# Two gained float32 tiles behind each output product instead of three, with the next norm's second half under a dense tile

## The chip, the cores and the metric

The kernel runs on one core of a Trainium2 chip. The metric is the device time of one execution in microseconds, lower is better.

## The reference

Two decoder layers over 512 prompt tokens and 8 sample tokens (one new token each), all in float32. Cut to what bears on the change:

```python
def rmsnorm(x, g):
    y = xf * lax.rsqrt(jnp.mean(xf * xf, axis=-1, keepdims=True) + EPS)
    return y * g

def decoder_layer(x, ...):
    m, mix_state = gated_parallel_mixer(rmsnorm(x, p['norm_mix_pre']), ...)   # ends in (...) @ w_out
    x = x + rmsnorm(m, p['norm_mix_post'])
    x = x + rmsnorm(cross_attention(rmsnorm(x, p['norm_x_pre']), ...), p['norm_x_post'])
    f, new_buf_ffn = conv_ffn(rmsnorm(x, p['norm_ffn_pre']), buf_ffn, p)
    x = x + rmsnorm(f, p['norm_ffn_post'])

def cross_attention(h, mem_k, mem_v, p):
    q = h @ p['w_xq']          # 8 tiles of 128 columns; softmax attention over 256 memory rows
    ...
    return o @ p['w_xo']

def conv_ffn(h, buf, p):
    a, g = split_cols(h @ p['w_ffn_in'], (D_FF, D_FF))   # 22 tiles each
    ...                        # causal convolution of a, silu, times g
    return (...) @ p['w_ffn_out']
```

So twice in each layer an output product (`w_out`, `w_xo`) is followed by a norm, a residual sum, a second norm of the new x, and at once by the next product (`w_xq`, `w_ffn_in`). These four places are what the change touches.

## The kernel before

Channels lie on the 128 partitions; the 520 tokens lie along the row in two halves of 260 (256 prompt tokens and 4 sample tokens each). A product is made tile by tile: one tile is 128 output columns, summed over the 128-row blocks k of the input.

**Dense tiles** (`dense`, `mm3`). Float32 accuracy is reached with the faster type float32r: weight and input are each split into a high and a low part, and three products (high x high, high x low, low x high) are summed. For 8 blocks and two halves that is 48 matmuls of 260 columns. `load_w` brings the raw weight in over SP's queue, ScalarE makes the high part (L169), VectorE the low part (L111). The pools hold three raw and four split weights. A dense tile's two halves lie in one `pd` buffer of PSUM, of which there are two; `ps` buffers (one bank) are four.

**Behind an output product** (`post`, `late`, `after_norm`). `post` evacuates the eight tiles of the output product into `mg`, sums their squares (`sums`), and forms the first norm's factor in two halves: `Rms` sums the squares over partitions with three small matmuls on TensorE (L267, "stat"), VectorE scales the sum (L250 `nms`), GpSimd raises it to the power -1/2 (L251 `ny`, "newton"), TensorE spreads it over partitions (L275), ScalarE copies it to SBUF (L277 `r`). `bulk(hf)` then makes the new x of one half on VectorE: 8 x (multiply by r, L335; add the residual `xo`, L338), written over `mg`. The second norm's factor r2 needs the squares of the new x: `squares(hf)` takes 8 squares on ScalarE and adds 7 of them (L296) on VectorE.

So that TensorE has work in this time, `after_norm` starts the next product with **three tiles in plain float32**: their weights are multiplied by the norm's gain on ScalarE (`load_wg`, 8 `wg` activations a tile), their input is the new x as it stands, unsplit, and the factor r2 is multiplied in at evacuation. One tile is 8 blocks x 2 halves = 16 matmuls (L407). Between the six (tile, half) groups `after_norm` calls `next(late)`, which emits the parts of `late` one after another: first norm's second half, `bulk(1)`, squares of half 0; r2 of half 0; squares of half 1, and so on; the splits of the new x for the dense tiles (`sph` on ScalarE, `spl` on VectorE) come last, ahead of r2's second half. Behind the three tiles the other tiles (`xq(3)`..., or `wf[NFF+1]`...) are dense.

A scheduler then sets each engine's order from these emissions; semaphores keep it. What the engines do is in that fixed order.

```python
                for k in range(8):
                    PE.matmul(ps[:, :HALF], ws[i][:, k], x[k][:, hf], start=(k == 0), stop=(k == 7))
                wait.append((i, ps, hf))
                next(late)
```

Of the kernel before, what the change touches and what calls it, by code (L numbers as in the profile page):

```python
# [23 lines left out]
NFF = DFF // P  # L24
# [41 lines left out]
def build(tc, I, O):  # L66
# [7 lines left out]
    with ExitStack() as es:  # L74
# [29 lines left out]
        G = nc.gpsimd  # L104
# [12 lines left out]
        def AV(t, hf=None):  # L117

            return t[:, :, :HALF] if hf is None else t[:, hf, :HALF]
# [75 lines left out]
                        PE.matmul(ps, a[:, k], b[:, hf], start=(first and k == 0 and i == 0),  # L195
                                  stop=(last and k == nk - 1 and i == 2))

        def dense(ap, xs):

            kt = len(xs)  # L200
            ps = PD()
            outs = [(ps[:, hf, :HALF], hf) for hf in range(2)]
            for k0 in range(0, kt, 8):
                k1 = min(kt, k0 + 8)
                mm3(load_w(ap[:, k0:k1], k1 - k0), xs[k0:k1], outs, k0 == 0, k1 == kt)
            return ps

        def window(aps, xs, mid=()):
# [91 lines left out]
        def post(w, xs_, gain, src, keep, nwin, nxt=None, final=False):  # L300

            sums = Sum()
            mg = [None] * 8

            def evac(m, ps, hf):
                if mg[m] is None:
                    mg[m] = C("mg")
                v = ps[:, :HALF] if hf is not None else AV(ps)  # L310
                sums.add(v, hf)
                act(AV(mg[m], hf), v, AF.Identity, scale=gain(m))

# [12 lines left out]
            rm, rm2 = {}, {}  # L326

            def stat(hf):
                rm[hf] = Rms(sums.acc, D, hf)

            def bulk(hf):
                for m in range(8):
                    x = AV(mg[m], hf)
                    E = G if not nxt and m in (2, 3) else V
                    E.tensor_tensor(out=x, in0=x, in1=AV(r, hf), op=ALU.mult)  # L335
                    if final and m % 2 == 0:
                        yo = C("yo")
                    E.tensor_tensor(out=yo[:, m % 2] if final else x, in0=x, in1=xo[m][hf], op=ALU.add)  # L338
                    if final and m % 2:
                        nc.sync.dma_start(out=keep[:, m - 1:m + 1, hf], in_=yo)  # L340

            def store():
                for m in range(8):
                    G.dma_start(out=keep[:, m], in_=mg[m])

            def squares(hf):
                for m in range(8):
                    sq2.add(AV(mg[m], hf), hf)

            def late():  # L350
                rm[1].spread(r)
                bulk(1)
                squares(0)
                yield
                rm2[0] = Rms(sq2.acc, D, 0)
                squares(1)
                yield
                rm2[0].spread(r2)
                yield
                rm2[1] = Rms(sq2.acc, D, 1, pd=rm2[0].pd)  # L360
                for m in range(8):
                    split_to(sp[m][0], sp[m][1], mg[m], nxt(m))
                yield
                rm2[1].spread(r2)
                yield
                store()
                yield

            mid = [lambda: None, lambda: stat(0), lambda: rm[0].spread(r)] if nwin == 1 else []
            for n, (i, ps, hf) in enumerate(window([w[m] for m in range(8 - nwin, 8)], xs_, mid)):  # L370
                evac(8 - nwin + i, ps, hf)
                if nwin > 1 and n == nwin:
                    stat(0)
                if nwin > 1 and n == nwin + 1:
# [12 lines left out]
            bulk(1)  # L387
            if not final:
                store()
            return mg  # L390

        def after_norm(aps, x, gain, late, evac):


            n = len(aps)
            ws = [load_wg(ap, 8, gain) for ap in aps]
            pd = None
            wait = []
            for j in range(2 * n):
                hf, i = divmod(j, n)  # L400
                if j < 4:
                    ps = PS()
                else:
                    pd = pd or PD()
                    ps = pd[:, j % 2]
                for k in range(8):
                    PE.matmul(ps[:, :HALF], ws[i][:, k], x[k][:, hf], start=(k == 0), stop=(k == 7))  # L407
                wait.append((i, ps, hf))
                next(late)
                while j >= n and wait and wait[0][2] == 0:  # L410
                    evac(*wait.pop(0))
            for v in wait:
                evac(*v)

        def drain(gen):
            while True:
# [119 lines left out]
        for L in range(DEPTH):  # L536
# [866 lines left out]
            def xq(m):  # L1403
                xq_evac(m, dense(I["w_xq"][L, m], xss), None)

            load_mem(0)
            for h in range(3):
# [3 lines left out]
                                          lambda m: pc("xpre", m)))  # L1411
            x_src = keep

            after_norm([I["w_xq"][L, m] for m in range(3)], x, lambda k: pc("xpre", k), late, xq_evac)
            s_load("mem_v", 0, 0)
            p_scores(0)
            s_scores(0, 0)
            s_load("mem_k", 3, 0)
# [92 lines left out]
            def ffn_g(j, ps, hf):  # L1511
                if j not in gth:
                    gth[j] = C("gg", (P, 512))
                tt(QV(gth[j], hf), PV(r, hf), PV(ps, hf), ALU.mult)
                tt(S8(g_s[:, j], hf), SV(r, hf), SV(ps, hf), ALU.mult)
                if hf is None and j > 1:
                    ffn_mul(j)

            def ffn_mul(j):
# [20 lines left out]
            wf = I["w_ffn_in"][L]  # L1540

            def first(i, ps, hf):
                (ffn_a, ffn_g, ffn_a)[i]((0, 0, 1)[i], ps, hf)

            after_norm([wf[0], wf[NFF], wf[1]], x, lambda k: pc("ffnpre", k), late, first)
            for j in range(1, NFF):
                if j > 1:
                    ffn_a(j, dense(wf[j], xss), None)
                ps = dense(wf[NFF + j], xss)
                ffn_g(j, ps, None)  # L1550
                if j == 1:
                    for i in range(2):
                        ffn_conv(i)
                        ffn_mul(i)
                if j == 8:
                    ffn_sample(0, 8)
                if 9 <= j < 17:
# [210 lines left out]
```

## Time and profile before

| | us |
|---|---|
| median of 3 runs | 3201.71 (3200.33 to 3203.3) |
| the profiled execution | 3205.31 |
| its span | 3203.5 |
| TensorE busy | 3160.6 (99%) |
| VectorE busy | 1949.0 (61%) |
| ScalarE busy | 1454.4 (45%) |
| GpSimd busy | 423.9 (13%) |

Busy times are those of the span, which is 1.8 us shorter than the execution's own time. A matmul's record is longer than the step to the next matmul, because matmuls overlap; what a matmul costs is read from the step between starts. A plain float32 matmul leaves two records, a float32r matmul one.

### The profile page before, as it was taken

To read this page: it belongs to the slowest core of one execution; us is meant where nothing else is said; L and a number is where in the kernel's file an instruction comes from. 1 tells how busy PE (TensorE), PEld (TensorE's weight loads), DVE (VectorE), ACT (ScalarE), POOL (GpSimd) and SP (SyncE) were. 2 spreads that over 40 slices of the span, in tenths; PEclk is the share of its full clock that TensorE was granted. 3 is DMA by queue.
4 is the path that set the end of the run, shared out by engine and by line. 5 is a ranking of instruction groups with operands and counts; after the bars stand their busy time and mean duration, and the time that the engine had idled before them with its cause. 6 is when DMAs were issued, how large, how long until landed. Compare 5 with 4: busy or idle time off the path is not lost. (4 is left out here: it accounts for less than half of the span.)

```text
span 3203.5 us, 64089 instructions
## 1 busy us (share of the span) xinstructions
PE 3160.6 (99%) x25878; PEld 3020.2 (94%) x25878; DVE 1949.0 (61%) x3773; ACT 1454.4 (45%) x3348; POOL 423.9 (13%) x762
## 2 busy tenths in 40 slices
PE   8999999999999999999999999999999999999998
PEld 7989999999999879999999899999999998899998
DVE  6665686777553537665286666777775436376643
ACT  5343566666433434333243445676673233433331
POOL 1100222122300101000020011222223001010001
PEclk9999999999999999999999999999999999999999
DMA  7322444444643553223263234444455336432231
GB/s 258 122 83 100 140 166 150 146 162 160 215 139 107 186 172 127 96 96 109 88 228 110 80 103 162 158 140 160 153 183 197 123 109 213 147 129 96 94 96 64
DMA packets 192168, 445.83 MB, mean 139 GB/s; under 512 B 26416, under 2 KB 78656, under 8 KB 191872
## 3 DMA queue, kind: packets, MB, share of 16 engines
q1 hardware_dynamic: 162736, 353.63, 33.0%
q0 software_dynamic: 27840, 86.01, 7.9%
q8 instruction: 203, 3.33, 0.4%
q10 hardware_dynamic: 1296, 2.11, 0.2%
q14 instruction: 93, 0.76, 0.1%
HBM read 377.81 MB, written 63.83 MB: 138 GB/s over the span
## 5 line engine op out<-in xcount | busy, mean ns | idle before, releaser
L169 ACT CAST wh<-wr 128x1024 fp32r<-128x1024 f32 (+1 forms) x484 | 503.4, 1041 | 1139.6 <-PE pd L195 763.9
L111 DVE TENSOR_TENSOR wl<-wr,wh 128x1024 fp32r<-128x1024 f32 (+1 forms) x484 | 591.4, 1223 | 523.3 <-ACT wh L169 514.4
L195 PE MATMUL pd<-xih,wh 128*128 128x260 f32 x3488 | 716.8, 287 | 3.2 <-ACT dd L108 3.2
L195 PE MATMUL pd<-xih,wl 128*128 128x260 f32 x3488 | 702.6, 283 | 0.0
L195 PE MATMUL pd<-xil,wh 128*128 128x260 f32 x3488 | 702.1, 283 | 0.0
L195 PEld LDWEIGHTS pd<-xih,wh 128*128 128x128 f32 x3488 | 536.8, 189 | 25.3 <-issue 19.2
L195 PEld LDWEIGHTS pd<-xih,wl 128*128 128x128 f32 x3488 | 537.7, 188 | 0.1
L195 PEld LDWEIGHTS pd<-xil,wh 128*128 128x128 f32 x3488 | 537.6, 189 | 0.1
L195 PE MATMUL pd<-sph,wh 128*128 128x260 f32 x1472 | 298.0, 284 | 0.0
L195 PE MATMUL pd<-spl,wh 128*128 128x260 f32 x1472 | 296.4, 283 | 0.0
L195 PE MATMUL pd<-sph,wl 128*128 128x260 f32 x1472 | 295.8, 282 | 0.0
L195 PEld LDWEIGHTS pd<-sph,wh 128*128 128x128 f32 x1472 | 226.8, 188 | 2.9 <-issue 2.7
L195 PEld LDWEIGHTS pd<-spl,wh 128*128 128x128 f32 x1472 | 227.9, 189 | 0.0
L195 PEld LDWEIGHTS pd<-sph,wl 128*128 128x128 f32 x1472 | 226.7, 188 | 0.1
L114 DVE SCALAR_TENSOR_TENSOR cv<-pb,hw,cv 128x512 f32<-128x512 f32 x192 | 143.6, 748 | 5.5 <-ACT cv L108 0.7
L251 POOL TENSOR_TENSOR ny<-nms,mhalf 128x3 f32<-128x3 f32 (+2 forms) x26 | 39.2, 1506 | 787.6 <-DVE nms L250 787.6
L195 PE MATMUL pd<-uh,wh 128*128 128x260 f32 x616 | 124.1, 283 | 0.0
L195 PE MATMUL pd<-uh,wl 128*128 128x260 f32 x616 | 123.9, 282 | 0.0
L195 PE MATMUL pd<-ul,wh 128*128 128x260 f32 x616 | 123.6, 282 | 0.0
L108 ACT ACTIVATE th<-cv 128x512 f32<-128x512 f32 x64 | 40.5, 633 | 154.4 <-DVE cv L114 133.0
L296 DVE TENSOR_TENSOR acc<-acc,sq 128x260 f32<-128x260 f32 (+1 forms) x126 | 61.8, 513 | 76.6 <-ACT sq L108 75.2
L195 PEld LDWEIGHTS pd<-ul,wh 128*128 128x128 f32 x616 | 95.1, 188 | 0.0
(425 smaller groups left out, 6052.1 us busy)
## 6 DMA issues: line engine op xcount, KB each, us to landing
wr<-in_w_in SPq DMA_DIRECT2D x218, 512.0 KB
wr<-in_w_ffn_in SPq DMA_DIRECT2D x88, 512.0 KB
hs<-in_ssm SPq DMA_DIRECT2D x64, 256.0 KB
csb<-csd SPq DMA_DIRECT2D x64, 256.0 KB
out_s_ssm<-hs POOLq DMA_DIRECT2D x64, 256.0 KB, 2.8
mem_k<-in_mem_k SPq DMA_DIRECT2D x64, 256.0 KB
wr<-in_w_ssm_out SPq DMA_DIRECT2D x32, 512.0 KB
mem_v<-in_mem_v SPq DMA_DIRECT2D x64, 256.0 KB
```

The costliest lines, as they stand in the source:

```text
L108: return A.activation(out, in_, f, **kw)
L111: return V.tensor_tensor(out=out, in0=a, in1=b, op=op)
L114: return V.scalar_tensor_tensor(out=out, in0=a, scalar=s, in1=b, op0=op0, op1=op1)
L169: A.copy(h[:, :nk], raw[:, :nk])
L195: PE.matmul(ps, a[:, k], b[:, hf], start=(first and k == 0 and i == 0), stop=(last and k == nk - 1 and i == 2))
L251: G.tensor_tensor(out=y, in0=ms, in1=mhalf[:, 0:n], op=ALU.pow)
L296: (E or V).tensor_tensor(out=AV(self.acc, h), in0=AV(self.acc, h), in1=AV(sq, h), op=ALU.add)
```

## The change

- `after_norm` takes **two** gained tiles instead of three (32 plain matmuls instead of 48 at each place), all four (tile, half) groups in `ps` buffers. The calls of `next(late)` stand inside the groups. It returns `rest`, which emits the last part of `late` and the evacuation of half 1.
- The third tile becomes a **dense** tile: `xq(2)`, or `wf[1]`. `dense` and its callers take `mid`: after 3 of 8 blocks it calls `rest`, that is, r2's second half (stat, newton, spread) and `store`.
- In `late` the splits of the new x come **first**, ahead of the squares of half 1; the squares of half 0 come before `bulk(1)`.
- The 7 additions of squares of each half go to **GpSimd** (`E=G`) instead of VectorE: 14 additions of 128x260 at each place, 56 in all.
- In the ConvFFN the convolution of tile 0 is emitted behind the dense tile `wf[1]`, and `ffn_g` of every tile calls `ffn_mul`.

The lines of the changed kernel are shifted: the additions of squares are L303, the stat L274, `nms` L257, `ny` L258, the spread L282, the copy of r L284, `bulk` L342 and L345, the stores L351.

```diff
-        def dense(ap, xs):
+        def dense(ap, xs, mid=None):
...
-                mm3(load_w(ap[:, k0:k1], k1 - k0), xs[k0:k1], outs, k0 == 0, k1 == kt)
+                h, l, nk = load_w(ap[:, k0:k1], k1 - k0)
+                if mid and k0 == 0:
+                    c = mid[0]
+                    mm3((h, l, c), xs[:c], outs, True, False)
+                    mid[1]()
+                    mm3((h[:, c:], l[:, c:], nk - c), xs[c:k1], outs, False, k1 == kt)
...
-                    sq2.add(AV(mg[m], hf), hf)
+                    sq2.add(AV(mg[m], hf), hf, G)
 
             def late():
+                squares(0)
                 rm[1].spread(r)
                 bulk(1)
-                squares(0)
                 yield
                 rm2[0] = Rms(sq2.acc, D, 0)
-                squares(1)
-                yield
-                rm2[0].spread(r2)
-                yield
-                rm2[1] = Rms(sq2.acc, D, 1, pd=rm2[0].pd)
                 for m in range(8):
                     split_to(sp[m][0], sp[m][1], mg[m], nxt(m))
+                squares(1)
+                yield
+                rm2[0].spread(r2)
+                yield
+                rm2[1] = Rms(sq2.acc, D, 1, pd=rm2[0].pd)
                 yield
                 rm2[1].spread(r2)
-                yield
                 store()
                 yield
...
+            for j in range(4):
+                hf, i = divmod(j, 2)
+                ps = out[i, hf] = PS()
                 for k in range(8):
                     PE.matmul(ps[:, :HALF], ws[i][:, k], x[k][:, hf], start=(k == 0), stop=(k == 7))
+                    if (j, k) in ((1, 3), (1, 7), (3, 1), (3, 7)):
+                        next(late)
+                    if (j, k) == (3, 1):
+                        for i2 in range(2):
+                            evac(i2, out[i2, 0], 0)
+
+            def rest():
                 next(late)
+                for i2 in range(2):
+                    evac(i2, out[i2, 1], 1)
...
-            after_norm([I["w_xq"][L, m] for m in range(3)], x, lambda k: pc("xpre", k), late, xq_evac)
+            rest = after_norm([I["w_xq"][L, m] for m in range(2)], x, lambda k: pc("xpre", k), late, xq_evac)
             s_load("mem_v", 0, 0)
+            xq(2, (3, rest))
             p_scores(0)
...
-            after_norm([wf[0], wf[NFF], wf[1]], x, lambda k: pc("ffnpre", k), late, first)
+            rest = after_norm([wf[0], wf[NFF]], x, lambda k: pc("ffnpre", k), late, first)
```

The orders below are those of the first layer; the second layer has the same ones.

GpSimd behind `w_out`, before: the newtons of the first norm's halves (`ny_13057`, `ny_13143`), the stores of the new x (`xd`), the newton of the second norm's half 0 (`ny_13245`).

```order
L251 TENSOR_TENSOR ny_13057<-nms_13056,mhalf 128x3
L251 TENSOR_TENSOR ny_13143<-nms_13142,mhalf 128x3
L344 DMA xd_12565<-mg_12621 128x520
L344 DMA xd_12565<-mg_12680 128x520
L344 DMA xd_12565<-mg_12740 128x520
```

The same in the changed kernel; `acc` is the sum of squares of the new x.

```order
L258 TENSOR_TENSOR ny_13057<-nms_13056,mhalf 128x3
L303 TENSOR_TENSOR acc_13182<-acc_13182,sq_13184 128x260
L303 TENSOR_TENSOR acc_13182<-acc_13182,sq_13187 128x260
L303 TENSOR_TENSOR acc_13182<-acc_13182,sq_13190 128x260
L303 TENSOR_TENSOR acc_13182<-acc_13182,sq_13193 128x260
L303 TENSOR_TENSOR acc_13182<-acc_13182,sq_13196 128x260
L303 TENSOR_TENSOR acc_13182<-acc_13182,sq_13199 128x260
L258 TENSOR_TENSOR ny_13143<-nms_13142,mhalf 128x3
L303 TENSOR_TENSOR acc_13182<-acc_13182,sq_13202 128x260
L351 DMA xd_12565<-mg_12621 128x520
```

Six additions now stand ahead of the newton of the first norm's half 1. The 7 additions of half 1 stand behind the stores, ahead of r2's second newton.

ScalarE in the changed kernel, around the end of the plain tiles (`sph` is the high part of the new x, `wh` that of a dense weight, `sq` a square of half 1):

```order
L169 CAST wh_13611<-wr_13609 128x1024
L108 ACTIVATE sph_12909<-mg_12958,prm_184 128x520
L108 ACTIVATE sph_12911<-mg_12988,prm_184 128x520
L108 ACTIVATE sph_12913<-mg_13018,prm_184 128x520
L108 ACTIVATE sq_13254<-mg_12680 128x260
L108 ACTIVATE sq_13257<-mg_12740 128x260
```

Before, the squares of half 1 stood ahead of all casts and splits of this stretch. Now all but one stand behind the last three splits and behind a cast that writes the buffer of a gained weight tile.

TensorE behind `w_xo` before, at r2's second half (`pd_14867` holds the second norm's sums and spreads):

```order
L267 MATMUL pd_14867<-cst,acc_14835 128x1 x3
L407 MATMUL pd_14953<-mg_14421,wg_14786 128x260
L407 MATMUL pd_14953<-mg_14481,wg_14786 128x260
L407 MATMUL pd_14953<-mg_14579,wg_14786 128x260
L407 MATMUL pd_14953<-mg_14609,wg_14786 128x260
L407 MATMUL pd_14953<-mg_14639,wg_14786 128x260
L275 MATMUL pd_14867<-cst,ny_14923 128x128 x2
L275 MATMUL pd_14867<-cst,ny_14923 128x4
L407 MATMUL pd_14953<-mg_14242,wg_14797 128x260
```

And in the changed kernel, at the end of the dense tile `wf[1]` (`pd_14963`) and the start of the next one (`pd_15055`):

```order
L195 MATMUL pd_14963<-sph_14559,wl_14967 128x260 x2
L274 MATMUL pd_14881<-cst,acc_14834 128x1 x3
L282 MATMUL pd_14881<-cst,ny_14960 128x128 x2
L282 MATMUL pd_14881<-cst,ny_14960 128x4
L195 MATMUL pd_15055<-sph_14545,wh_15058 128x260 x2
```

The scheduler put stat and spread of half 1 behind the whole dense tile, with nothing between them; behind `w_out` two score matmuls of the cross-attention stand between them. The next dense tile takes a third `pd` buffer where there are two.

## Rows read from the trace of the kernel before

**Rows 1.** The page's first part: busy time, share and instructions of each engine.
```profile
PE 3160.6 (99%) x25878; PEld 3020.2 (94%) x25878; DVE 1949.0 (61%) x3773; ACT 1454.4 (45%) x3348; POOL 423.9 (13%) x762
```
**Rows 2.** TensorE's waits, whole program: engine, line, waited for: us, times, longest.
```profile
PE pd L275 <- POOL ny L251: 7.2, 9, 1.3
...
PE pd L195 <- ACT dd L108: 3.2, 1, 3.2
```
**Rows 3.** Timeline of TensorE behind `w_out`, layer 0: start us, us, what, [idle before].
```profile
1061.63 0.83 PE L275 MATMUL pd<-cst,ny 128*128 128x128 f32 x6 [1.06 <-POOL ny L251]
1062.32 9.45 PE L407 MATMUL ps<-mg,wg 128*128 128x260 f32 x42
...
1073.76 0.83 PE L275 MATMUL pd<-cst,ny 128*128 128x128 f32 x6 [0.35 <-POOL ny L251]
...
1076.00 2.44 PE L407 MATMUL pd<-mg,wg 128*128 128x260 f32 x10
```
**Rows 4.** Timeline of TensorE in the first dense tile behind it.
```profile
1083.18 0.40 PE L195 MATMUL pd<-sph,wh 128*128 128x260 f32 x2
1083.42 0.40 PE L195 MATMUL pd<-spl,wh 128*128 128x260 f32 x2
```
**Rows 5.** Timeline of VectorE in the same place.
```profile
1053.12 0.77 DVE L335 TENSOR_TENSOR mg<-mg,r 128x260 f32<-128x260 f32 x2 [0.20 <-ACT r L277]
1053.81 0.76 DVE L338 TENSOR_TENSOR mg<-mg,xo 128x260 f32<-128x260 f32 x2
...
1058.91 0.15 DVE L250 TENSOR_SCALAR nms<-pd 128x3 f32<-128x3 f32 x1
...
1062.90 0.77 DVE L335 TENSOR_TENSOR mg<-mg,r 128x260 f32<-128x260 f32 x2 [2.04 <-ACT r L277]
```
**Rows 6.** Timeline of ScalarE in the same place.
```profile
1051.78 0.40 ACT L108 ACTIVATE wg<-wr,prm 128x128 f32<-128x128 f32 x1 [0.47 <-PE ps L195]
...
1057.26 2.27 ACT L108 ACTIVATE sq<-mg 128x260 f32<-128x260 f32 x7
...
1073.05 1.04 ACT L169 CAST wh<-wr 128x1024 fp32r<-128x1024 f32 x1 [4.18 <-PE ps L407]
1074.63 0.38 ACT L277 COPY r<-pd 128x260 f32<-128x260 f32 x1 [0.53 <-PE pd L275]
1074.90 2.59 ACT L108 ACTIVATE sph<-mg,prm 128x520 fp32r<-128x520 f32 x4
```
**Rows 7.** VectorE and GpSimd share one `bulk` behind the first layer's `w_ffn_out`: timeline.
```profile
1599.36 1.32 DVE L335 TENSOR_TENSOR mg<-mg,r 128x260 f32<-128x260 f32 x2 [0.93 <-ACT r L277]
1599.40 1.88 POOL L335 TENSOR_TENSOR mg<-mg,r 128x260 f32<-128x260 f32 x2 [1.50 <-ACT r L277]
...
1601.25 1.83 POOL L338 TENSOR_TENSOR mg<-mg,xo 128x260 f32<-128x260 f32 x2
...
1603.63 0.76 DVE L338 TENSOR_TENSOR mg<-mg,xo 128x260 f32<-128x260 f32 x2
```
**Rows 8.** Groups of GpSimd's instructions, by form: | busy us, mean ns of one | idle before.
```profile
L296 POOL TENSOR_TENSOR acc<-acc,sq 128x520 f32<-128x520 f32 x30 | 39.9, 1330 | 57.9 <-ACT sq L108 56.8
...
L338 POOL TENSOR_TENSOR mg<-mg,xo 128x260 f32<-128x260 f32 x4 | 3.7, 931 | 0.0
```
**Rows 9.** A newton with a VectorE subtraction right behind its `nms`: timeline.
```profile
1608.28 0.14 DVE L250 TENSOR_SCALAR nms<-pd 128x3 f32<-128x3 f32 x1
1608.35 1.21 DVE L111 TENSOR_TENSOR wl<-wr,wh 128x1024 fp32r<-128x1024 f32 x1
...
1608.50 2.06 POOL L251 TENSOR_TENSOR ny<-nms,mhalf 128x3 f32<-128x3 f32 x1 [5.42 <-DVE nms L250]
```
**Rows 10.** A newton with VectorE nearly idle: timeline of GpSimd.
```profile
1049.16 0.99 POOL L251 TENSOR_TENSOR ny<-nms,mhalf 128x3 f32<-128x3 f32 x1 [96.46 <-DVE nms L250]
```
**Rows 11.** Stretches: length, busy PE, PEld, DVE, ACT, POOL, TensorE's granted clock, DMA.
```profile
76.00:79.00 3.00, 0.02 (x1) 0.03 (x1) 0.64 (x1) 1.71 (x3) 0.00 (x0) 1.00 0.29 116
79.00:82.00 3.00, 3.00 (x15) 3.00 (x16) 3.00 (x6) 2.62 (x4) 0.00 (x0) 0.57 0.43 141
```

More of the change, by code (lines that the diff above doesn't have):

```diff
@@ L204, in dense @@
                 k1 = min(kt, k0 + 8)
[L205 removed]
+                h, l, nk = load_w(ap[:, k0:k1], k1 - k0)
[4 more added lines that the diff above has]
+                    mm3((h[:, c:], l[:, c:], nk - c), xs[c:k1], outs, False, k1 == kt)
+                else:
+                    mm3((h, l, nk), xs[k0:k1], outs, k0 == 0, k1 == kt)
             return ps
@@ L347, in squares @@
                 for m in range(8):
-                    sq2.add(AV(mg[m], hf), hf)
+                    sq2.add(AV(mg[m], hf), hf, G)
             def late():
+                squares(0)
                 rm[1].spread(r)
                 bulk(1)
-                squares(0)
                 yield
                 rm2[0] = Rms(sq2.acc, D, 0)
+                for m in range(8):
+                    split_to(sp[m][0], sp[m][1], mg[m], nxt(m))
                 squares(1)
@@ L360, in late @@
                 rm2[1] = Rms(sq2.acc, D, 1, pd=rm2[0].pd)
-                for m in range(8):
-                    split_to(sp[m][0], sp[m][1], mg[m], nxt(m))
                 yield
                 rm2[1].spread(r2)
-                yield
                 store()
@@ L392, in after_norm @@
         def after_norm(aps, x, gain, late, evac):
-            n = len(aps)
             ws = [load_wg(ap, 8, gain) for ap in aps]
[L397 to L405, printed above, removed]
+            out = {}
+            for j in range(4):
+                hf, i = divmod(j, 2)
+                ps = out[i, hf] = PS()
                 for k in range(8):
                     PE.matmul(ps[:, :HALF], ws[i][:, k], x[k][:, hf], start=(k == 0), stop=(k == 7))
-                wait.append((i, ps, hf))
+                    if (j, k) in ((1, 3), (1, 7), (3, 1), (3, 7)):
[4 more added lines that the diff above has]
+            def rest():
                 next(late)
[L410 to L413, printed above, removed]
+                for i2 in range(2):
+                    evac(i2, out[i2, 1], 1)
+            return rest
         def drain(gen):
@@ L1401, in s_split, with xq @@
                     V.tensor_copy(SV(oxs[m][1]), S8(sl[:, m]))
-            def xq(m):
-                xq_evac(m, dense(I["w_xq"][L, m], xss), None)
+            def xq(m, mid=None):
+                xq_evac(m, dense(I["w_xq"][L, m], xss, mid), None)
             load_mem(0)
@@ L1515, in ffn_g @@
                 tt(S8(g_s[:, j], hf), SV(r, hf), SV(ps, hf), ALU.mult)
-                if hf is None and j > 1:
+                if hf is None:
                     ffn_mul(j)
@@ L1542, in first @@
             def first(i, ps, hf):
-                (ffn_a, ffn_g, ffn_a)[i]((0, 0, 1)[i], ps, hf)
-            after_norm([wf[0], wf[NFF], wf[1]], x, lambda k: pc("ffnpre", k), late, first)
+                (ffn_a, ffn_g)[i](0, ps, hf)
+            rest = after_norm([wf[0], wf[NFF]], x, lambda k: pc("ffnpre", k), late, first)
             for j in range(1, NFF):
-                if j > 1:
-                    ffn_a(j, dense(wf[j], xss), None)
+                ffn_a(j, dense(wf[j], xss, (3, rest) if j == 1 else None), None)
+                if j == 1:
+                    ffn_conv(0)
+                    ffn_mul(0)
                 ps = dense(wf[NFF + j], xss)
                 ffn_g(j, ps, None)
[L1551 to L1554, printed above, removed]
                 if j == 8:
```

## The prediction

> **What bounds the kernel now.** The page's first part comes first: TensorE is busy 99% of the span [rows 1]. Whatever makes it run longer or wait is therefore time, and work taken off the other engines is not, unless TensorE waits for it. Next TensorE's waits: what it lost behind the output products is the spread (L275) waiting for a newton, 7.2 us in 9 waits [rows 2]. The timeline of one place shows them: 1.06 us ahead of the first norm's second spread, 0.35 us ahead of the second norm's first [rows 3]. The last spread has no wait: its newton lies under ten plain matmul records of 2.44 us [rows 3]. Then the other engines in the same microseconds: VectorE makes half 0 of the new x from 1053.12 (two operations in 0.69 us, 0.34 each) and waits 2.04 us for the spread before half 1 [rows 5]; ScalarE does seven squares in 2.27 us, 0.32 each [rows 6]. So before the change additions at VectorE's 0.34 keep up with the squares.
>
> The sum is made for the place behind `w_out` in layer 0 and applied to all four; the two behind `w_xo` differ in one term. A time is + when the kernel gets longer.
>
> **T1, the tile that changes kind: −1.5 a place.** Forty-two plain records take 9.45 us, 0.225 each [rows 3]; a tile has 16 matmuls of two records, 7.2 us. In a dense tile two starts lie 0.24 apart (1083.18, 1083.42) [rows 4], 0.12 each, and 48 make 5.7 us.
>
> **T2, half 0 of the new x: +2.8.** The third tile's gain operations (0.40 each [rows 6]) leave ScalarE and its cast and subtraction (1.04 [rows 6], 1.21 [rows 9]) come ahead of the first norm's spread and `bulk(0)`; I take 1.0 us of delay to the start of `bulk(0)`. The larger part is the additions. Before, GpSimd did nothing in `bulk(0)`; now six additions stand ahead of `ny` of half 1, and some five fall into VectorE's 16 operations. What one costs VectorE is seen where the two engines share a `bulk`: VectorE's six operations from 1599.36 to 1603.63 took 4.27 us where six at 0.34 take 2.04, while four on GpSimd ran (pairs of 1.88 and 1.83) [rows 7]. The excess is 2.2 us, 0.55 for each GpSimd operation. Five make 2.75. `nms` of half 1 stands between the operations of this stretch as before, and the interval from `nms` (1058.91 [rows 5]) to the spread (1061.63 [rows 3]), 2.7 us, stays: newton waits for its turn behind an addition in place of running slowly. TensorE has to fill the time with two more plain matmuls than before, 0.9 us by four records, which takes off nearly what the 1.0 adds. Net 2.75, rounded to 2.8. Ends: 0, if the additions take nothing from VectorE, and 4.65, if each holds it for its whole 0.93 [rows 8].
>
> **T3, half 0 of the second norm: 0.** Its spread waited 0.35 [rows 3]. Now six store issues stand ahead of its newton on GpSimd, but its `nms` stands behind `bulk(1)` on VectorE too, so nothing is later because of them. The squares and additions of half 0 are done before `bulk(1)` is, since the newton that `bulk(1)` waits for stands behind six of the additions. The same transfers are issued on SP's queue, a place or two apart in order. ScalarE loses eight gain operations and VectorE 14 additions of 0.34 at each place; neither bounds [rows 1], so 0. The convolution of the FFN's tile 0 goes to VectorE behind a dense tile of 5.7 us, on an engine that is 39% idle [rows 1]: 0.
>
> **T4, the sums of half 1 behind the dense tile: +3.2.** The order has nothing between the dense tile's last matmul and the stat. Let E be the end of the last plain matmul. ScalarE's cast there writes a gained tile's buffer, so it must wait for E, as a cast does now (idle 4.18 us for L407, then 1.04 [rows 6]). Behind it stand three splits (four take 2.59, 0.65 each [rows 6]) and then seven squares (0.32). The first square is done about E + 3.4: 1.0 of cast, 1.9 of splits, 0.4 of square, 0.1 of semaphores. The squares then come every 0.32 and GpSimd can't follow: an addition of 520 elements takes 1.33 us there [rows 8], half of it 0.67, with the step to the next 0.7. Seven make 4.9; half a microsecond more I take for one that VectorE's low splits hold up. The stat can run at E + 8.8; the dense tile ends at E + 5.7. The wait is 3.1 to 3.2. Ends: 0.2, if GpSimd does an addition at VectorE's pace (seven at 0.34, E + 5.9), and 4.8, if each takes the 0.93 of the other 128x260 form [rows 8]. One sentence from the Trainium skill beside it: the page "GPSIMD Engine Reference", section "Elementwise — side-by-side cycle accounting", gives 4497 ns for an addition of 2048 float32 elements; scaled to 260 that is, as an estimate, 0.57 us, by which T4 would be 2.3 and the whole sum some 3.6 us less, and no row of before shows this size alone.
>
> **T5, the last newton without cover: +1.5 behind `w_out`, +2.9 behind `w_xo`.** Its stat and spread now follow each other. From stat to spread are `nms` (0.14) and `ny`, which took 2.06 with a VectorE subtraction `wl` right behind `nms` [rows 9], as the order has it here too, and 0.99 with VectorE nearly idle [rows 10]. I take 2.06, with semaphores 2.4. Behind `w_out` two score matmuls stand between, 0.9 if they cost what two plain ones do (four records [rows 3]): 1.5 left. Behind `w_xo` there are none, and the next dense tile asks for a `pd` buffer that comes free when ScalarE has copied r2 (0.38 [rows 6], 0.5 with semaphores): 2.9. Ends: 0.5 and 1.8 with 0.99; 1.9 and 3.3 with 0.4 more than 2.06.
>
> **T6, TensorE's clock: +1.3 a place.** In a 3 us stretch in which TensorE was busy 0.02 us the granted clock was still 1.00; in the next 3 us, all busy, it was 0.57 [rows 11]. Those three microseconds lie mostly at the lower of the two levels, 1.2 GHz, and lost 0.43 x 3 = 1.3 us. The new idle stretches (3.2, then 1.5 to 2.9) are as long as that one (TensorE's single wait of 3.2 us on L195 [rows 2] among them). Ends: 0 and 2.6 (both waits lose it).
>
> **The sum.** Behind `w_out` −1.5 + 2.8 + 3.2 + 1.5 + 1.3 = 7.3; behind `w_xo` 8.7; two of each: **+32**. The profiled execution took 3205.3, 3.6 over the median of 3201.7; +32 on the median is **3234**. All low ends together: −0.8 and 0.5, twice, −0.6. All high ends: −1.5 + 4.65 + 4.8 + 1.9 + 2.6 = 12.5 and 13.9, twice, +53, 3255.
>
> **The rivals.**
>
> *The additions take nothing from VectorE* (T2 is 0, and the half microsecond in T4 goes): 3.9 and 5.3 a place, +18, **3220**. For it: an addition writes one buffer and reads two of its own, so nothing in the program ties it to `bulk`. Against it: the slowed VectorE of [rows 7], whose operations were tied to GpSimd's by nothing either.
>
> *The additions hold VectorE altogether*: 4.65 in place of 2.75 in T2, +1.9 at four places, +40, **3241**. For it: GpSimd's 0.93 an operation; against it: the 0.55 that VectorE lost for each [rows 7]. The Trainium skill, "SBUF — State Buffer", section "Who interferes with whom", states this rule: the ports that VectorE and GpSimd share are an exclusive lock, so of two such operations the later waits for the other's end. The row agrees that there is interference, but with a smaller price than a whole operation.
>
> *Faster*: additions on GpSimd that keep the squares' pace of 0.32 and leave VectorE alone. It decides at about 0.35 us an addition: then T4 is 0.2 at most, T2 is 0, and with newtons of 0.99 the spread waits of 1.06 and 0.35 [rows 3] go as well. A place is −1.5 − 1.4 + 0.5 = −2.4 or, behind `w_xo`, −1.1; together −7, **3195**. Against it: 0.67 for half of the 520-element form [rows 8], about twice the 0.35.
>
> *No change*: every unknown at its low end, with the waits of before left as they are: **3201**. It needs GpSimd fast, newtons short and the clock kept, three rows against it at once.
>
> **How the numbers follow.** The forecast of +32 (24 to 39 by its own ends) has 0.62; nothing taken from VectorE 0.13; a whole hold 0.10; faster 0.09; no change 0.06. A measurement of this kernel can tell about 0.2%, 6.4 us. Faster by more: 0.09; within: 0.06; slower by more: 0.85. The range leaves out the faster case and no change, and the upper ends of the others: it reaches from 3212, below the rival without the hold, to 3246, above the one with the whole hold.
>
> **What would show each step.** T1: 16 fewer L407 matmuls at each place. T2: VectorE's `bulk(0)` with operations of 0.6 to 0.9 while L303 runs on GpSimd; with 0.38 each the rival without the hold is right. T4: four waits of some 3 us of L274 for an addition of GpSimd (or for a square, if the splits are longer than I took), and 128x260 additions of 0.65 to 0.7; below 0.4 the faster rival is right. T5: spreads (L282) that wait 1.5 us or more for `ny`, twice without other work, and the next dense tile idle behind the copy of r2. T6: the granted clock near 0.5 behind these waits. The prediction is wrong if L274 waits for nothing, or if the waits are there but TensorE's busy time falls by more than they cost.

## The result: 51.6 us slower, beyond the forecast's range

| | before | changed |
|---|---|---|
| median, us | 3202.51 (3200.33 to 3204.12) | 3254.07 (3251.64 to 3256.9) |
| profiled execution, us | 3205.31 | 3251.64 |
| span, us | 3203.5 | 3249.9 |
| ratio of the runs | | 1.0165 (1.0153 to 1.0177) |

The forecast was 3234 with a range from 3212 to 3246. The direction was right, the size was not: +51.6 us instead of +32.

The page's first part of the changed kernel, which answers to [rows 1]: TensorE is busy 15.6 us more although 6 us of matmuls were saved (matmuls at the lower clock, below, last longer and count as busy), and its share fell.

```profile
PE 3176.2 (98%) x25942; PEld 3033.3 (93%) x25942; DVE 1948.0 (60%) x3713; ACT 1449.0 (45%) x3320; POOL 465.6 (14%) x818
```

TensorE's waits of the changed kernel (us, times, longest), against [rows 2]. The spreads' wait doubled from 7.2 us; three new ones stand beside it.

```profile
PE pd L282 <- POOL ny L258: 14.8, 9, 2.4
PE pd L274 <- POOL pb L1496: 7.8, 2, 3.9
PE pd L274 <- POOL acc L303: 7.7, 2, 3.9
...
PE ps L407 <- DVE mg L345: 6.0, 10, 1.5
```

The timeline of TensorE behind `w_out`, layer 0, against [rows 3]. Two idle stretches: plain matmuls wait for `bulk(0)` and then the spread for its newton (1.49 and 1.80 us); behind the dense tile the stat waits 3.87 us for the sum of squares. What follows each is slow: six records of a spread take 1.44 us instead of 0.83 [rows 3], and four score records 2.05 at 1085.61 but 1.11 at 1089.25.

```profile
1059.14 1.14 PE L407 MATMUL ps<-mg,wg 128*128 128x260 f32 x4 [1.49 <-DVE mg L345]
1062.09 1.44 PE L282 MATMUL pd<-cst,ny 128*128 128x128 f32 x6 [1.80 <-POOL ny L258]
...
1084.31 1.44 PE L274 MATMUL pd<-cst,acc 128*128 128x1 f32 x6 [3.87 <-POOL acc L303]
1085.61 2.05 PE L1295 MATMUL ps<-km,qx 128*128 128x256 f32 x4
1087.97 1.41 PE L282 MATMUL pd<-cst,ny 128*128 128x128 f32 x6 [0.31 <-POOL ny L258]
1089.25 1.11 PE L1295 MATMUL ps<-km,qx 128*128 128x256 f32 x4
```

The same behind `w_xo`, layer 0: 2.39 us for the first norm's newton, then 3.89, 2.24 and 0.47 in a row.

```profile
1226.49 1.44 PE L282 MATMUL pd<-cst,ny 128*128 128x128 f32 x6 [2.39 <-POOL ny L258]
...
1251.78 0.83 PE L274 MATMUL pd<-cst,acc 128*128 128x1 f32 x6 [3.89 <-POOL pb L1496]
1254.85 1.44 PE L282 MATMUL pd<-cst,ny 128*128 128x128 f32 x6 [2.24 <-POOL ny L258]
1256.76 0.80 PE L195 MATMUL pd<-sph,wh 128*128 128x260 f32 x2 [0.47 <-ACT r L284]
```

Stretches of the changed kernel (length, busy PE, PEld, DVE, ACT, POOL, TensorE's granted clock, DMA share, GB/s). From the waits on the clock is at its lower level, 1.2 GHz: behind `w_out` for 3.4 us from 1061.9 and again for 6.8 us from 1082.4, behind `w_xo` for 10.2 us from 1225.8, among them the 9 us from 1227 on, in all of which TensorE was busy.

```profile
1061.00:1064.00 3.00, 1.91 (x8) 1.81 (x9) 0.02 (x1) 0.38 (x1) 1.74 (x3) 0.65 0.53 175
...
1085.00:1088.00 3.00, 2.69 (x9) 1.79 (x9) 1.33 (x2) 0.00 (x0) 1.82 (x1) 0.50 0.00 0
1227.00:1236.00 9.00, 9.00 (x28) 7.55 (x27) 7.60 (x20) 2.65 (x5) 5.37 (x10) 0.50 0.57 218
```

The same two places of the kernel before, 45 us from about the first plain matmul on, at a granted clock of 1.00 throughout:

```profile
1055.00:1100.00 45.00, 43.59 (x280) 38.05 (x282) 33.24 (x85) 20.57 (x45) 9.11 (x11) 1.00 0.54 190
1210.00:1255.00 45.00, 43.46 (x282) 39.56 (x281) 38.57 (x94) 22.39 (x41) 11.52 (x18) 1.00 0.49 161
```

**Where the time went.** For each place I added TensorE's waits, and separately what it lost at 1.2 GHz: over stretches of half a microsecond, busy time x (1 − granted clock). "Grew" is measured apart from both: from the first plain matmul of a place to that of the next one (for the last place, to the span's end).

| place | grew | waits, before and after | lost to the clock | tile (T1) | sum |
|---|---|---|---|---|---|
| `w_out`, layer 0 | 9.1 | 1.4, 7.7 | 3.9 | −1.5 | 8.7 |
| `w_xo`, layer 0 | 14.7 | 1.5, 10.3 | 7.0 | −1.5 | 14.3 |
| `w_out`, layer 1 | 11.6 | 1.4, 7.7 | 6.1 | −1.5 | 10.9 |
| `w_xo`, layer 1 | 14.1 | 1.5, 10.3 | 5.1 | −1.5 | 12.4 |
| all | 49.5 | 5.9, 35.9 | 22.1 | −6 | 46.1 |

Ahead of the first place the changed kernel's execution was 3.1 us shorter, which makes the 46.4 us between the spans; between the medians it is 51.6, as the profiled execution of before was 2.8 us above its median and that of the changed kernel 2.4 below. So 30 us are waits and 22 us the clock, which was never low in these places before; the tile gives 6 back, and 3.4 us of the 49.5 are in none of these rows. The forecast had 32.8 us of delays and 5.2 us of clock.

### The profile page after: what moved, and what is told of

Read it like the earlier page. It is cut to its first block, busy times and chain, and to the rows that moved or that the text cites. A ratio compares the mean times of both kernels' runs of the same rounds, so it can differ in the third digit from the quotient of the medians.

```text
span 3249.9 us, 64213 instructions
## 1 busy us (share of the span) xinstructions
PE 3176.2 (98%) x25942; PEld 3033.3 (93%) x25942; DVE 1948.0 (60%) x3713; ACT 1449.0 (45%) x3320; POOL 465.6 (14%) x818
## 3 DMA queue, kind: packets, MB, share of 16 engines
q1 hardware_dynamic: 162736, 353.63, 32.8%
## 5 line engine op out<-in xcount | busy, mean ns | idle before, releaser
L195 PE MATMUL pd<-sph,wh 128*128 128x260 f32 x1536 | 314.3, 285 | 0.9 <-ACT r L284 0.9
L195 PE MATMUL pd<-spl,wh 128*128 128x260 f32 x1536 | 311.6, 284 | 0.0
L195 PE MATMUL pd<-sph,wl 128*128 128x260 f32 x1536 | 308.8, 282 | 0.0
L195 PEld LDWEIGHTS pd<-sph,wh 128*128 128x128 f32 x1536 | 238.5, 189 | 4.3 <-issue 2.7
L195 PEld LDWEIGHTS pd<-sph,wl 128*128 128x128 f32 x1536 | 238.1, 189 | 0.0
L195 PEld LDWEIGHTS pd<-spl,wh 128*128 128x128 f32 x1536 | 237.9, 189 | 0.1
L258 POOL TENSOR_TENSOR ny<-nms,mhalf 128x3 f32<-128x3 f32 (+2 forms) x26 | 36.1, 1390 | 738.3 <-DVE nms L257 738.2
L303 POOL TENSOR_TENSOR acc<-acc,sq 128x260 f32<-128x260 f32 (+1 forms) x86 | 88.8, 1032 | 119.3 <-ACT sq L108 115.2
L195 PEld LDWEIGHTS pd<-uh,wh 128*128 128x128 f32 x616 | 95.1, 188 | 0.0
```

What stands on the lines that cost most here:

```text
L258: G.tensor_tensor(out=y, in0=ms, in1=mhalf[:, 0:n], op=ALU.pow)
L303: (E or V).tensor_tensor(out=AV(self.acc, h), in0=AV(self.acc, h), in1=AV(sq, h), op=ALU.add)
```

## The experiments

"Sum" in this table is worked out as above: waits less the 5.9 of before, plus what the clock took, plus useless matmuls (those that some runs add for the test) at 0.225 us a record, less 6 us where there are two plain tiles. The runs of before on the same chip had medians of 3200.2 to 3201.39.

| run | median, us | ratio to before, interval | waits | clock | sum | over before |
|---|---|---|---|---|---|---|
| before_newton_2 | 3210.34 | 1.0028 (1.0017 to 1.0039) | 9.2 | 3.4 | +6.7 | +9.0 |
| before_newton_4 | 3220.77 | 1.0061 (1.0044 to 1.0077) | 15.8 | 10.8 | +20.7 | +19.4 |
| before_newton_4_fill | 3213.06 | 1.0032 (1.0018 to 1.0046) | 5.5 | 0 | +10.4 | +11.7 |
| three_tiles_gpsimd | 3226.08 | 1.0075 (1.0060 to 1.0091) | 20.6 | 9.1 | +23.8 | +24.8 |
| fill_second | 3255.59 | 1.0165 (1.0150 to 1.0180) | 20.9 | 15.7 | +46.3 | +55.4 |
| fill_both | 3244.24 | 1.0132 (1.0116 to 1.0149) | 14.1 | 4.9 | +35.9 | +44.0 |
| half0_on_vector | 3241.05 | 1.0124 (1.0109 to 1.0139) | 28.3 | 13.0 | +29.4 | +40.9 |
| half1_on_vector | 3246.76 | 1.0145 (1.0130 to 1.0160) | 31.0 | 22.3 | +41.4 | +46.6 |
| both_on_vector | 3236.56 | 1.0105 (1.0090 to 1.0120) | 24.4 | 14.5 | +27.0 | +35.3 |
| squares_first | 3231.58 | 1.0091 (1.0076 to 1.0106) | 24.9 | 8.0 | +20.9 | +30.3 |
| vector_and_squares_first | 3213.61 | 1.0039 (1.0026 to 1.0051) | 13.0 | 0 | +1.1 | +12.3 |
| dense_undivided | 3254.83 | 1.0167 (1.0151 to 1.0182) | 35.9 | 23.1 | +47.1 | +53.4 |

### Does a wait cost more than itself?

The first three runs leave the change aside: in the kernel before they make one wait of each place longer and touch nothing else. In `newton` of the first norm's half 1, behind `nms`:

```diff
+            for _ in range(slow):          # 1, or 3
+                G.tensor_tensor(out=S("nyd", (P, n), 4), in0=ms, in1=mhalf[:, 0:n], op=ALU.pow)
             G.tensor_tensor(out=y, in0=ms, in1=mhalf[:, 0:n], op=ALU.pow)
```

**before_newton_2** (one useless power).

> The kernel before with one useless power more on GpSimd (about 0.9 us) ahead of the newton of the first norm's half 1 at the four places: the wait of 1.06 us ahead of that spread becomes about 2.0 us, nothing else changes. If a wait costs only itself: +4 us, 3205. If the clock falls behind a wait of 2 us as it did behind the waits of 1.8 to 2.4 us in the changed kernel: 1.7 us or more a place beside it, 3211 to 3215, with the granted clock at 0.50 behind each.

The wait became 1.88 to 1.92 us. Behind it the clock fell at two of the four places and stayed at the other two. The stretches right behind the wait, first in layer 0 behind `w_out`, then behind `w_xo`:

```profile
1059.00:1062.00 3.00, 3.00 (x10) 2.37 (x9) 2.72 (x8) 1.23 (x4) 1.07 (x2) 0.59 0.01 3
...
1216.00:1219.00 3.00, 3.00 (x15) 2.59 (x15) 3.00 (x10) 1.52 (x4) 1.49 (x3) 1.00 0.16 64
```

Ten records in 3 us at the one place, fifteen at the other. The time, +9.0 us, lies just below the second expectation: two of the four dips are in it.

**before_newton_4** (three).

> The same with three useless powers: a wait of about 3.8 us, as long as the changed kernel's second one. If a wait costs only itself: +11 us, 3212. If the clock falls behind it: another 7 to 16 us (1.7 to 4 a place), 3219 to 3228.

The wait is 3.5 us, and the clock fell at all four places. Timeline of TensorE and stretches behind `w_out`, layer 0:

```profile
1063.14 1.44 PE L277 MATMUL pd<-cst,ny 128*128 128x128 f32 x6 [3.51 <-POOL ny L253]
```

```profile
1062.00:1065.00 3.00, 1.86 (x7) 1.78 (x8) 0.00 (x0) 0.38 (x1) 1.09 (x2) 0.53 0.13 51
1065.00:1068.00 3.00, 3.00 (x8) 2.36 (x7) 2.97 (x9) 1.23 (x4) 1.16 (x2) 0.50 0.05 21
```

9.9 us of waiting became 19.4 us of time; the sum by the rows is 20.7. So a wait at this spot costs about twice its length, and the second half of it is paid behind it.

**before_newton_4_fill** lays 6 useless plain matmuls a place into that wait, ahead of the spread, which overwrites what they wrote:

```diff
             def late():
+                for _ in range(6):
+                    PE.matmul(rm[1].pd[:, 1, :HALF], ident, AV(mg[0], 0), start=True, stop=True)
                 rm[1].spread(r)
```

> The run with three useless powers, and 6 useless plain matmuls (2.7 us) on TensorE in that wait, overwritten by the spread. The end of the wait does not move. If the loss beside the wait is the clock's: the granted clock stays 1.00 and the time is that of the wait alone, 3212, 7 to 16 us below the run without the useless matmuls. Rival (the loss is something else): no difference, or slower.

3213.06: 7.7 us less for 10.8 us more of matmuls. Timeline and stretch of the same place: 1.38 us of wait are left, the spread takes 0.83 again, and the clock is at 1.00.

```profile
1060.23 0.83 PE L277 MATMUL pd<-cst,ny 128*128 128x128 f32 x6 [1.38 <-POOL ny L253]
```

```profile
1061.00:1064.00 3.00, 3.00 (x18) 2.65 (x17) 2.49 (x8) 1.14 (x3) 0.84 (x2) 1.00 0.00 0
```

That settles what most of the loss beside the wait is: work that did nothing but keep TensorE from idling kept the clock up and gave 7.7 us of it back.

### The clock in the changed kernel

```diff
+            def fill(n, ps, src):
+                for _ in range(n):
+                    PE.matmul(ps[:, 1, :HALF], ident, src, start=True, stop=True)
             def late():
                 squares(0)
+                fill(4, rm[1].pd, AV(mg[0], 0))          # fill_both alone
                 rm[1].spread(r)
...
+                fill(8, rm2[0].pd, AV(mg[0], 1))
                 rm2[1] = Rms(sq2.acc, D, 1, pd=rm2[0].pd)
+                fill(4, rm2[0].pd, AV(sq2.acc, 1))
                 rm2[1].spread(r2)
```

In both, and in dense_undivided, the dense tile is left whole and this part comes behind it.

**fill_second.**

> The changed kernel with useless matmuls that keep TensorE busy in the second idle stretch of each place: 8 plain matmuls of 260 columns (0.45 us each) behind the dense tile, ahead of the stat, and 4 between stat and spread; their result is overwritten by the spread. Theory A: the forecast missed the clock; after the idle stretch the matmuls run at 1.2 GHz for some 4 to 5 us, and that costs about 2.2 us a place beside the wait itself. Then the work added costs almost nothing (it lies in waits of 3.9 and 1.8 to 2.2 us), the granted clock stays 1.00 between the dense tile and the next one, and the time is about 9 us below the changed kernel's 3254: 3245 (3242 to 3249). Rival B: the waits are the whole cost and the dips come regardless of them: 3252 to 3260, with the dip still there.

A miss. No gain: 3255.59. The eight matmuls lie in the wait, but the stat waits 1.24 us behind them all the same, since the squares' sum came later (the seven additions ahead of it took 7.05 us behind `w_out`, 6.16 in the changed kernel), and the clock fell again at all four places:

```profile
1081.00 3.68 PE L355 MATMUL pd<-mg,cst 128*128 128x260 f32 x16
1085.92 0.83 PE L270 MATMUL pd<-cst,acc 128*128 128x1 f32 x6 [1.24 <-POOL acc L299]
```

```profile
1086.00:1089.00 3.00, 3.00 (x12) 2.51 (x13) 0.16 (x1) 0.00 (x0) 0.87 (x1) 0.63 0.20 76
```

The dips took 15.7 us instead of 22.1, and waits and useless matmuls together 42.5 instead of 35.9: the one pays for the other. So the dips are not held off by making a wait short; 1.24 us ahead of stat, newton and spread were enough here.

**fill_both.**

> As the run before, and 4 more useless matmuls (1.8 us) ahead of the first norm's second spread, in the wait for its newton. Theory A: the first dip goes too; at it the matmuls ran at 1.2 GHz for 3.1 us behind w_out and 9.5 us behind w_xo, half of that lost, 12 us in all: 3233 (3229 to 3239). Rival: the 1.5 us of waiting for the new x that is left there is enough for the clock to fall: no gain over the run before, 3245.

3244.24, 11 us below fill_second with 7.2 us more of useless matmuls, and 10 us below the changed kernel with 28.8 us of them. The first dips are gone at all four places; of the second ones two were left, 4.9 us. The gain is half of what was expected, because waits and useless matmuls together are 7 us longer than the waits alone.

**dense_undivided** has none of them.

> The changed kernel with the dense tile left whole, and stat and spread of half 1 emitted behind it. The order of TensorE, where the scheduler had put both behind the whole tile already, is nearly the same; 3250 to 3258, as the changed kernel. It is also what the runs with useless matmuls in the second wait stand against. Rival: the position of the stat in the text matters, 3 us or more of difference.

3254.83: the three-of-eight position of the stat in the text does nothing, since the scheduler puts it behind the whole tile in either case.

### Which engine adds, and in which order

The additions moved back to VectorE, one half at a time:

```diff
-                    sq2.add(AV(mg[m], hf), hf, G)
+                    sq2.add(AV(mg[m], hf), hf, G if hf else V)     # half0_on_vector
+                    sq2.add(AV(mg[m], hf), hf, V if hf else G)     # half1_on_vector
+                    sq2.add(AV(mg[m], hf), hf)                     # both_on_vector
```

First what they do in the changed kernel: VectorE and GpSimd behind `w_out`, layer 0.

```profile
1054.61 1.84 DVE L345 TENSOR_TENSOR mg<-mg,xo 128x260 f32<-128x260 f32 x2
1056.38 1.83 DVE L342 TENSOR_TENSOR mg<-mg,r 128x260 f32<-128x260 f32 x2
1058.14 1.29 DVE L345 TENSOR_TENSOR mg<-mg,xo 128x260 f32<-128x260 f32 x2
1059.35 0.15 DVE L257 TENSOR_SCALAR nms<-pd 128x3 f32<-128x3 f32 x1
1059.42 1.21 DVE L111 TENSOR_TENSOR wl<-wr,wh 128x1024 fp32r<-128x1024 f32 x1
```

```profile
1054.27 4.53 POOL L303 TENSOR_TENSOR acc<-acc,sq 128x260 f32<-128x260 f32 x5 [7.60 <-ACT sq L108]
1059.69 1.53 POOL L303 TENSOR_TENSOR acc<-acc,sq 128x260 f32<-128x260 f32 x1 [0.88 <-ACT sq L108]
1061.18 0.85 POOL L258 TENSOR_TENSOR ny<-nms,mhalf 128x3 f32<-128x3 f32 x1
...
1078.10 6.16 POOL L303 TENSOR_TENSOR acc<-acc,sq 128x260 f32<-128x260 f32 x7 [6.03 <-ACT sq L108]
```

VectorE's last six operations of `bulk(0)` took 4.74 us up to `nms` instead of 2.04, beside five additions: 2.7 us, 0.54 for each. Then the newton stands behind a sixth addition of 1.53 us, which lies beside the subtraction `wl`.

**half0_on_vector.**

> The changed kernel with the additions of half 0 back on VectorE, those of half 1 on GpSimd. Theory A (an addition on GpSimd slows VectorE's bulk(0), so that plain matmuls and the newton come late, and the clock falls behind that): the waits of 1.0 to 1.5 us for the new x and of 1.8 to 2.4 us for the newton shrink to 1 us in all, the first dip goes, and the time is 20 to 25 us lower: 3231. The second waits stay at 3.9 us. Rival (the additions do not hold VectorE, the cast and the subtraction ahead of bulk(0) are what is late): the waits stay, 3250 to 3256.

The same operations without additions on GpSimd, 0.68 us for two and 2.03 for six:

```profile
1057.67 0.76 DVE L345 TENSOR_TENSOR mg<-mg,xo 128x260 f32<-128x260 f32 x2
1058.35 0.76 DVE L342 TENSOR_TENSOR mg<-mg,r 128x260 f32<-128x260 f32 x2
```

The first waits shrank from 3.5 and 3.7 us to 1.4 and 1.5, and the first dip went, as theory A had it; that the additions slow VectorE is shown. The time fell by 13 us, not by 20 to 25. By the rows the waits gave back 7.6 us and the clock 9.1; 3.7 of these 16.7 us do not show in the time, and which part of it holds them is not shown. The second dips took 13.0 us in all, nearly the 12.3 of the changed kernel, but otherwise spread: in layer 0 4.2 us behind `w_out` and 3.0 behind `w_xo` (2.3 at either in the changed kernel), in layer 1 2.3 behind `w_out` (4.4). How long a dip lasts differs between runs of nearly the same order.

**half1_on_vector.**

> The changed kernel with the additions of half 1 on VectorE, those of half 0 on GpSimd. If GpSimd's pace sets the wait ahead of the stat (the term T4: seven additions at 0.7 to 0.9 us behind squares at 0.32), the wait falls from 3.9 to 0.3 us and the second dip goes with it: 22 us lower, 3232. If it is set by the splits that stand ahead of the squares (first square at the end of the plain tiles + 3.4 us, the dense tile 5.7 us), VectorE's additions end at + 6 or a little later: 1.5 to 2.5 us of wait are left, and with the newton behind it the dip may stay: 5 to 9 us lower, 3245 to 3249.

The second answer holds: the wait only fell to 1.9 us (behind `w_out`, where a score matmul now has it) and 2.4 us, and the dip stayed. The row has four waits, of which two stood in before's list already, with 4.2 us.

```profile
PE pd L274 <- DVE acc L303: 9.1, 4, 2.4
```

**both_on_vector.**

> The changed kernel with all additions of squares on VectorE, everything else as changed. By the traces of the two halves run apart: the first waits shrink to 1.6 us a place (as with half 0 on VectorE), the second ones to 3.3 us behind w_out and 5.1 us behind w_xo (as with half 1 there), and a dip of the clock is left behind the second wait only, 1.7 to 3.7 us a place. Against before: -6 for the tile, +17 for waits, +7 to +15 for dips: +18 to +26, 3219 to 3227. Rival (GpSimd's additions are the whole loss, and order and tile are free): 3196 to 3204.

A miss by 10 us: 3236.56, with waits and dips about as expected (24.4 and 14.5 us), and 8 us more than their sum. Moving the additions back undoes a third of the loss: the order and the tile hold the rest.

**squares_first** keeps GpSimd and turns two lines of `late` round; **vector_and_squares_first** has VectorE's additions as well:

```diff
+                squares(1)
                 for m in range(8):
                     split_to(sp[m][0], sp[m][1], mg[m], nxt(m))
-                squares(1)
```

> The changed kernel with the squares of half 1 ahead of the splits, as before the change; additions on GpSimd. If the splits that stand ahead of the squares are what makes the second wait: no wait of 3.9 us ahead of the stat, but short waits of the dense tile for its splits (some 1.4 us a place); the first waits and their dip stay. 15 to 22 us below the changed kernel: 3233 to 3239. Rival (GpSimd's pace sets it): the wait only moves, 3248 to 3256.

3231.58, 22.5 us below the changed kernel. The wait of 3.87 us ahead of the stat is gone although GpSimd adds; the stat stands inside the dense tile. In its place are short waits of the dense tile for low splits (and, at one place, a single wait of 3.2 us for a newton, behind which the clock did not fall, as the last two rows show):

```profile
1081.22 0.51 PE L195 MATMUL pd<-spl,wh 128*128 128x260 f32 x2 [0.76 <-DVE spl L114]
...
1083.85 0.72 PE L274 MATMUL pd<-cst,acc 128*128 128x1 f32 x6
...
1238.73 0.83 PE L282 MATMUL pd<-cst,ny 128*128 128x128 f32 x6 [3.19 <-POOL ny L258]
```

```profile
1239.00:1242.00 3.00, 3.00 (x19) 2.71 (x19) 1.23 (x2) 0.06 (x1) 2.95 (x5) 1.00 0.73 258
```

> Both edits together: two plain tiles and the dense tile, additions on VectorE, squares ahead of splits. Then no single wait is above 1.2 us; some 4 us of short waits a place behind w_out, 5 behind w_xo, against 1.4 before. -6 for the tile, +13 for waits: 3209 if the clock stays, 3212 to 3216 if it falls once or twice. Rival (with both undone the tile alone is left, -6 and no wait): 3194 to 3198, faster than before.

3213.61, no dip, no wait of a place above 1.2 us; still 12.3 us above before, and the rival (the tile alone is left, faster than before) fell. The listed waits explain only +1.1, and the 3209 that was expected for a clock that stays is missed by 4 us. The stretch of the dense tile behind `w_out`, layer 0, and three of its rows:

```profile
1071.00:1079.00 8.00, 6.50 (x48) 5.67 (x47) 7.99 (x17) 4.80 (x8) 0.00 (x0) 1.00 0.48 151
```

```profile
1071.24 0.40 PE L195 MATMUL pd<-sph,wh 128*128 128x260 f32 x2
1072.18 0.51 PE L195 MATMUL pd<-spl,wh 128*128 128x260 f32 x2 [0.54 <-DVE spl L114]
1072.52 0.40 PE L195 MATMUL pd<-sph,wl 128*128 128x260 f32 x2
```

VectorE is busy all 8 us and TensorE 6.5: the splits of the new x, which before lay under the third plain tile, now bound the dense tile that took its place. The waits list counts too little for such a stop. From 1071.24 the next pair starts after 0.94 us instead of 0.24, and the one behind it after 0.34: 0.80 us more, of which the list has 0.54. The last matmul's record, 0.28 us long where the step is 0.12, covers the first 0.16 of the stop, and one matmul behind it takes 0.22. Four such stops, two of them under 0.15 us and so not listed, cost 2.6 us by the steps and 1.36 by the list. At four places that is some 5 us of the missing 11; the rest I have not traced.

**three_tiles_gpsimd** is the kernel before with GpSimd's additions (`sq2.add(AV(mg[m], hf), hf, G)`) and nothing else.

> The kernel before with one edit: its additions of squares of the new x on GpSimd. Its order puts five of them ahead of the newton of the first norm's half 1 and into bulk(0). If GpSimd's additions are harmful wherever they stand: waits of 2 to 2.7 us ahead of the first norm's second spread and about 2 us ahead of the second norm's first, 16 to 20 us, and a dip of the clock behind the longer of them at 1.7 to 4.7 us a place: 3225 to 3238. Rival (three plain tiles cover them): 3201 to 3206.

```profile
PE pd L275 <- POOL ny L251: 21.9, 9, 4.5
```

Waits of 3.8 to 4.5 us ahead of the first norm's second spread, all four followed by a dip. The third plain tile covers nothing there, because it comes later.

## Why the prediction was wrong, step by step

- **T2** (+2.8): mechanism and price were right. VectorE's delay was 2.7 us, 0.54 an addition against 0.55 from [rows 7]. The waits up to the first norm's second spread became 2.4 us longer than before behind `w_out` and 2.6 behind `w_xo`. Single operations out of the merged rows above show where the price comes from:

```profile
1055.37 0.80 POOL L303 TENSOR_TENSOR acc<-acc,sq 128x260 f32<-128x260 f32 x1
1055.50 0.96 DVE L345 TENSOR_TENSOR mg<-mg,xo 128x260 f32<-128x260 f32 x1
1056.24 0.81 POOL L303 TENSOR_TENSOR acc<-acc,sq 128x260 f32<-128x260 f32 x1
```

  VectorE's operation ends 0.29 us behind the addition that it overlaps (1056.46 and 1056.17), and the next addition ends 0.59 behind that (1057.05). So the two engines take turns, one operation each in 0.88 us, and VectorE loses 0.54 of it. The sixth addition, too, ends (1061.22) 0.59 us behind the end of the `wl` that it lies beside (1060.63). The Trainium skill's rule of an exclusive lock ("SBUF — State Buffer", section "Who interferes with whom") agrees with these turns. The rival of a whole hold had the price wrong: a GpSimd record of 0.93 us beside VectorE contains its own waiting.
- **T3** (0): nearly; the wait of the second norm's first spread, 0.35 and 0.45 us, is gone.
- **T4** (+3.2): 3.87 to 3.89. Seven additions took 6.16 us, 0.88 each, where the forecast had 4.9 and 0.5 for a delay: that is the difference. The mean over the program is

```profile
L303 POOL TENSOR_TENSOR acc<-acc,sq 128x260 f32<-128x260 f32 x56 | 48.9, 872 | 61.9 <-ACT sq L108 58.8
```

  The estimate of 0.57 us from the Trainium skill's page "GPSIMD Engine Reference" (section "Elementwise — side-by-side cycle accounting") is further off, even against the addition of 0.73 us at 1251.00 (below), which runs beside nothing. The low end, 0.2 us at VectorE's pace, was wrong: half1_on_vector took away only 1.5 to 2 us of the wait, squares_first all of it. The splits ahead of the squares make as much of it as GpSimd's pace. The squares come where the forecast had them, behind three splits (ScalarE, behind `w_out`, layer 0):

```profile
1075.73 1.98 ACT L108 ACTIVATE sph<-mg,prm 128x520 fp32r<-128x520 f32 x3
1077.60 2.28 ACT L108 ACTIVATE sq<-mg 128x260 f32<-128x260 f32 x7
```

  Behind `w_xo` the waits list names `pb` L1496: a memset of 0.10 us that GpSimd does between the additions. The wait is for the last addition all the same, as GpSimd's timeline there shows:

```profile
1250.86 0.10 POOL L1496 MEMSET pb<- 128x2 f32 x1
1251.00 0.73 POOL L303 TENSOR_TENSOR acc<-acc,sq 128x260 f32<-128x260 f32 x1
```

- **T5** (+1.5 and +2.9): 0.31 and 2.24 + 0.47. Behind `w_xo` right. Behind `w_out` the score matmuls covered more, because they ran at 1.2 GHz (2.05 us instead of 0.9 to 1.1): that time stands under the clock.
- **T1** (−1.5): the matmuls are gone as counted, but the runs with two plain tiles all cost 5 to 11.5 us more than their sums, those with three at most 2.3. So the tile gave less than 6 us, or something as large is lost beside it. Part of it is how the sums count: a stop takes 0.16 us more than its listed wait and up to 0.1 in the step behind it (vector_and_squares_first), and at the four places the runs with two plain tiles have 22 to 31 listed waits, those with three 4 to 8. As an estimate from these numbers that makes 2 to 6 us; the rest stays open.
- **T6** (+1.3, at most +2.6): **this step failed.** Measured are 3.9, 7.0, 6.1 and 5.1 us, 22.1 in all and not 5.2; the 17 us between are nearly what lacks from the forecast's 32 to the 49.5 of the places. (The waits were 2.8 us less than forecast, and 3.4 us are in no row.) It had one stretch of before as its price [rows 11], since "the new idle stretches (3.2, then 1.5 to 2.9) are as long as that one", and counted only the second waits. That stretch of 3 us cut the dip off; up to 83 us the clock was low as well, and the dip cost 0.43 x 4 = 1.7 us and not 1.3:

```profile
79.00:83.00 4.00, 4.00 (x20) 4.00 (x21) 4.00 (x8) 3.33 (x5) 0.00 (x0) 0.57 0.51 155
```

  The first waits (1.5 and 1.8 us, 2.4 behind `w_xo`) I took for a delay of 2.8 us without asking what the clock does behind them: it fell behind them at all four places. And a dip cost up to 4.75 us, where the highest end allowed 1.3 for each. The range's upper end, 3246, was set by a rival that says nothing of the clock; all high ends together, 3255, would have held the result.

The rival of a whole hold would have been nearer with 3241, for a wrong reason: VectorE lost 0.54 us an addition and not 0.93. The rivals "faster" and "no change" are refuted by the waits above.

No version beat the kernel before. Of those with two plain tiles, the one with VectorE's additions and squares first came nearest, at 1.0039.

## What to carry to other kernels

A wait of TensorE is worth its length and what the clock takes behind it: before_newton_4 paid 19.4 us for 9.9 us of new waiting. Not every wait has a dip behind it, so a forecast needs a range for it. So count idle stretches one by one, also those that a sum of delays hides, and ask of each what runs behind it and at which clock. Work that is moved from VectorE to GpSimd is not gone from VectorE: each addition there still took 0.54 us of an operation beside it, where it had cost 0.34 itself. And a queue's order (what stands ahead of the squares or of the newton) may cost more than the engine that does the work.

## What was not expected of the hardware

- The clock fell behind waits of 1.9 us at two of four places, of 3.5 us at four of four, of 1.22 to 1.24 us ahead of the stat at six of eight (fill_second, fill_both), and of 1.38 us behind plain matmuls at none (before_newton_4_fill). Nor did it fall behind the one wait of 3.19 us in squares_first. Which of the equal ones it follows, these runs don't tell.
- Dips lasted from 3.4 to 10.2 us, with TensorE busy in most of it: in the changed kernel 9 us of plain matmuls behind a wait of 2.39 us ran at 1.2 GHz.
- An addition of 128x260 on GpSimd took 0.72 to 0.73 us with VectorE idle. Beside VectorE's operations of the same size the two engines took turns, one operation each in 0.88 us, where VectorE alone does one in 0.34.
